# Attention of a two-layer trunk on one core: TensorE's order written out by hand, scores two units ahead, an even fill, the compressed branch in stages

## The chip, the cores and the metric

One core of one Trainium2 chip. The metric is the device time of one execution of the whole kernel, in microseconds (us), the median of several runs. All data are float32; some matmul operands are held as a pair of fp32r tiles ("high" and "low" part), so that a product is taken in three or two passes.

## The reference

Two layers, 256 tokens, width 1024. Layer 0 is native sparse attention, layer 1 an S5 state-space mixer; each is gated by silu(z) and added to the residual stream. Only layer 0 matters here; cut to its core:

```python
q, kc, vc, ks, vs, kw, vw, gates, z = split(rmsnorm(x) @ w_in)   # 16 heads of 64, 4 groups
k_cmp, v_cmp = compress(kc), compress(vc)      # silu(blocks of 32 tokens @ w1) @ w2: 15 blocks
for each block of 64 queries:
    p_c = softmax(q k_cmp - slope * distance)  # compressed branch
    p_s = softmax(q k_sel - slope * distance)  # selected blocks (at 256 tokens: all of them)
    p_w = softmax(q k_win - slope * distance)  # window of 512: all of them
    o = g0 * p_c v_cmp + g1 * p_s v_sel + g2 * p_w v_win
h1 = x + (o * silu(z)) @ w_out
```

Layer 1 then takes `h1` through its own projections and a scan, whose tables depend on its parameters alone ("ep" and "bbT" below) and are made beside the attention.

## The kernel before

**What is computed where.** The query, gate, key and value projections of layer 0 come as jobs of steps: `PRE` (line 36) lists those done ahead of the attention (values, keys, gates, the two inputs of the compression, and the queries q0 of group 0). `FILL` (line 37) lists the jobs that run beside it: the queries q1 to q3, the z gates z0 to z3 (eight steps each, of two fp32 matmuls, 128x256), `m` (the compression's hidden layer, eight steps) and `c` (its output, two steps). A job's name given several times stands for one step at a time, a name given once for all its steps.

**The attention** runs over 24 units (line 1045): 4 groups, 2 pairs of heads, 3 units a pair. Unit u=0 is the first 128 queries of both heads, u=1 and u=2 are the second 128 queries of one head each. Each unit has:

- `scores` (line 933): TensorE multiplies q and k into one of two "su" banks; VectorE adds the distance term and takes the row minimum (L955), ScalarE takes the exponential (L959), GpSimd two small steps on the sums (L964, L965), VectorE the reciprocal (L966), ScalarE scales (L968). The result is `pt`, two buffers.
- `transposes` (line 970): four TensorE transposes of `pt` (L973), copied by VectorE to `pT` (L975, three buffers).
- `values` (line 977): for u=0 and u=2 the products with v (L986) into one "ob" bank; with u=0 also the compressed branch's product (L1005), if its weights are there. Otherwise the pair is put aside by a copy (`aside`, L1012), and `complete` and `gated` finish it later.

The compressed branch of a group (`cmp_branch`, line 890) is scores (L894), a copy to `sct`, transposes of it (L900) and a softmax that goes from VectorE to GpSimd (L906), ScalarE, VectorE, GpSimd (L910), VectorE and GpSimd (L912, L913); `cmp_transpose` (line 916) transposes its result back on TensorE (L919).

**The loop** (lines 1127 to 1141) takes for unit n: the scores of unit n+1, three steps of the background (`adv(PACE)`), fill steps, out-projection steps if the fill is used up (`out_some`), one step of the compressed branch (`cmp_ready`), values of unit n-1, fill again, transposes of unit n. Up to unit 5 there are four fill steps a unit, then three (`RATES`), so the 66 steps are used up some five units before the end.

**The background** (`s5_gen`, line 484) makes layer 1's tables: 24 GpSimd steps for `ep` (lines 567 to 576), then 16 rounds of three GpSimd steps for `bbn` (two buffers), each closed by four TensorE transposes (L604) and a ScalarE copy (L606) in the same step.

**The out-projection** with `w_out0` is 8 steps (first 512 columns: `out_step`; the others: `gen1`) of 12 fp32r matmuls, 128x512. Each needs its weights split by ScalarE (`wh`, L207) and GpSimd (`wl`, L209), and the gated outputs split by `oz_split` (`ozh`, `ozl`, L1038 and L1039). `ozl` takes one of four buffers ("actT") that the normalised input `xn`, which all fill steps read, belongs to as well.

**The order.** Each engine runs its own queue in a fixed order. The order is made ahead of time by a planner: it takes instructions by priority (their place in the program) as soon as its own estimate of times says that they can start. Only inside a block `tc.manual_schedule(engines=...)` do the named engines keep the order of the program. In the kernel before, the attention's loop stands outside such a block; the out-projection's rest (lines 1150 to 1159) stands in one for TensorE.

Of the kernel before, what the change touches and what calls it, by code (L numbers as in the profile page):

```python
# [8 lines left out]
F32 = mybir.dt.float32  # L9
# [24 lines left out]
BGOFF = 0  # L34
WCOL = {"ck": 1024, "cv": 1280, "k0": 1536, "v0": 1792, "k1": 2048, "v1": 2304}
PRE = "v0 v1 k0 k1 gt ck cv q0"
FILL = "q1 q1 m q1 q1 m q1 q1 m q1 q1 m m m m m c z0 q2 z1 q3 z2 z3"
RATES = (4, 3)
SLOT_L = [4 * lh + l4 for l4 in range(4) for lh in range(2)]


# [5 lines left out]
def kernel(  # L47
# [52 lines left out]
    def bank(tag="b1", bufs=None):  # L100
        return phase["pool"].tile([P, 512], F32, tag=tag, name=tag, bufs=bufs or phase["bufs"])
# [4 lines left out]
    def bg_bank():  # L106
        return psb.tile([P, 512], F32, tag="bg", name="bg")
# [32 lines left out]
    def bb_part(g):  # L140
        for g0, t_ in reversed(bbT):
            if g >= g0:
                return t_, g - g0
# [238 lines left out]
    def ptt(o, a, b_, op=ALU.mult):  # L382
        PL.tensor_tensor(o, a, b_, op=op)  # L383
# [100 lines left out]
    def s5_gen():  # L484
# [100 lines left out]
        xp_ = xm.__enter__()  # L585

        GB = 4
        for q in range(GS // GB):
            gs = slice(q * GB, (q + 1) * GB)
            sh = [P, GB, L, 16]  # L590
            bbn = xp_.tile(sh, F32, tag="bbn", name="bbn", bufs=2)
            bbt = xp_.tile(sh, F32, tag="bbt", name="bbt", bufs=1)

            def pb_(ri):
                return pws[:, ri, :, gs].rearrange("p l g -> p g l").unsqueeze(3).to_broadcast(sh)

            ptt(bbn, b1c[:, gs].unsqueeze(2).to_broadcast(sh), pb_(0))
            yield
            ptt(bbt, b2c[:, gs].unsqueeze(2).to_broadcast(sh), pb_(1))
            yield  # L600
            ptt(bbn, bbn, bbt, ALU.add)
            bt = bg_bank()
            for i in range(4):
                T.transpose(bt[:, i * P:(i + 1) * P], bbn[:, i].rearrange("p l c -> p (l c)"), ident)  # L604
            o, g_ = bb_part(q * GB)
            A.activation(o[:, g_:g_ + 4].rearrange("p g x -> p (g x)"), bt, AF.Copy)  # L606
            yield
        xm.__exit__(None, None, None)
        sh_ld["bbar"] = True
        while "taps" not in sh_ld:  # L610
# [36 lines left out]
    def adv(n, offset=BGOFF):  # L647
        with tc.high_priority(-offset):
            for _ in range(n):
                next(bg, None)  # L650
# [103 lines left out]
    def cmp_steps():  # L754

        b = bank("cm", 1)
        for t in range(2):
            T.transpose(b[:, t * P:(t + 1) * P], hid[:, t * P:(t + 1) * P], ident)
        V.tensor_copy(hidT.rearrange("p t v x -> p (t v x)"), b[:, :256])
        b = bank("cm", 1)  # L760
        for t in range(2):
            T.matmul(b[:, :G0 * NB], w2[:, 0, t].rearrange("p u d -> p (u d)"), hidT[:, t, 0],
                     start=(t == 0), stop=(t == 1))
        V.tensor_scalar(kcT[:, :, 0:NB], b[:, :G0 * NB].rearrange("p (g n) -> p g n", n=NB), 0.5, None, op0=ALU.mult)
        dump("kcT", kcT)

        V.tensor_reduce(vm, ident[:R0 * NB, :R0 * NB].rearrange("p (r n) -> p r n", n=NB), axis=AX.X, op=ALU.add)
        V.tensor_scalar(vm, vm, 0.5, None, op0=ALU.mult)
        for t in range(2):
            V.tensor_copy(hidTv4[:, t], hidT[:, t, 1].rearrange("p (g n) -> p g n", n=NB).unsqueeze(2)  # L770
                          .to_broadcast([P, G0, R0, NB]))
        yield
        b = bank("cm", 1)
        for g in range(G0):
            for t in range(2):
                T.matmul(b[:R0 * NB, g * 64:g * 64 + 64], hidTv4[:, t, g].rearrange("p r n -> p (r n)"),
                         w2[:, 1, t, 0], start=(t == 0), stop=(t == 1))
        for r in range(R0):
            V.tensor_scalar(vc2[:, :, r], b[:R0 * NB, :256].rearrange("p (g d) -> p g d", g=G0), vm[:, r:r + 1],
                            None, op0=ALU.mult)  # L780
        dump("vc2", vc2)
        yield
# [85 lines left out]
            done.add(name)  # L868

    n_steps = {}  # L870
    STEPS = {"gt": 8, "v0": 1, "v1": 1, "m": 8, "c": 2}
    for i, name in enumerate(PRE.split()):
        if i == 1:
            b = bank("cm", 1)
# [15 lines left out]
    def cmp_branch(g, qs):  # L890

        b = bank("cm", 1)
        for r in range(R0):
            T.matmul(b[32 * r:32 * r + 32, :S], kcT[:, g], qs[r % 2][:, r // 2].bitcast(F32), start=True, stop=True,  # L894
                     tile_position=(0, 32 * r))
        sct = awp.tile([P, S], F32, tag="sct", name="sct", bufs=1)
        V.tensor_copy(sct, b[:, :S])
        b = bank("cm", 1)
        for j in range(NQ):
            T.transpose(b[:, j * P:(j + 1) * P], sct[:, j * P:(j + 1) * P], ident)  # L900
        sc = awp.tile([P, NQ, R0, NB], F32, tag="sc", name="sc", bufs=2)
        V.scalar_tensor_tensor(sc, b[:, :S].rearrange("p (j r n) -> p j r n", j=NQ, r=R0)[:, :, :, 0:NB], 0.125,
                               cbias[:, :, 4 * g:4 * g + 4], op0=ALU.mult, op1=ALU.add)
        mx = smp.tile([P, NQ, R0], F32, tag="mx", name="mx")
        V.tensor_reduce(mx, sc, axis=AX.X, op=ALU.max)
        PL.tensor_tensor(sc, sc, mx.unsqueeze(3).to_broadcast([P, NQ, R0, NB]), op=ALU.subtract)  # L906
        A.activation(sc, sc, AF.Exp)
        sm = smp.tile([P, NQ, R0], F32, tag="sm", name="sm")
        V.tensor_reduce(sm, sc, axis=AX.X, op=ALU.add)
        PL.tensor_scalar(sm, sm, 1e-30, None, op0=ALU.max)  # L910
        V.reciprocal(sm, sm)
        PL.tensor_tensor(sm, sm, gate[:, :, 4 * g:4 * g + 4], op=ALU.mult)  # L912
        PL.tensor_tensor(sc, sc, sm.unsqueeze(3).to_broadcast([P, NQ, R0, NB]), op=ALU.mult)  # L913
        return sc
# [11 lines left out]
    class Pair:  # L926
# [6 lines left out]
        def scores(self, u):  # L933
# [10 lines left out]
            if u == 0:  # L944
                for hf in range(2):
                    self.b8[hf] = awp.tile([P, S], F32, tag="b8", name="b8", bufs=4)
                    A.activation(self.b8[hf], dist, AF.Copy, scale=-8.0 * _slope(4 * g + 2 * self.pr + hf))
            pt = awp.tile([P, 4, P], F32, tag="pt", name="pt", bufs=2)
            self.pt[u] = pt
            parts = []  # L950
            for i, hf in enumerate(heads):
# [18 lines left out]
        def transposes(self, u):  # L970
            tb = bank("tu", 1)
            for i in range(4):
                T.transpose(tb[:, i * P:(i + 1) * P], self.pt[u][:, i], ident)  # L973
            self.pT[u] = awp.tile([P, 4, P], F32, tag="pT", name="pT", bufs=3)
            V.tensor_copy(self.pT[u].rearrange("p a q -> p (a q)"), tb)  # L975

        def values(self, u, pcT):
# [30 lines left out]
        def aside(self):  # L1008

            i = 2 * self.g + self.pr  # L1010
            part = ozf[:, 6 + i] if i < 2 else awp.tile([P, S], F32, tag="part", name="part", bufs=2)
            A.activation(part, self.ob[:, :S], AF.Copy, scale=0.5)  # L1012
            self.ob, self.half = part, True

# [25 lines left out]

    fill = FILL.split()
    seq = []
    for name in fill:
        seq += [name] * (1 if fill.count(name) > 1 else STEPS.get(name, KT))
    units = [(g, pr, u) for g in range(G0) for pr in range(2) for u in range(3)]
    owed = 0.0
    pairs, cmps, pcT = {}, {}, {}

    def fill_next():
        if seq:  # L1050
            step(seq.pop(0))
# [2 lines left out]
        while key not in done:  # L1054
            fill_next()

    def fill_some(n):
        nonlocal owed
        owed += 0.5 * RATES[n >= 6]
        while owed >= 1.0:  # L1060
            owed -= 1.0
            fill_next()

    def stage_s(n):
        if n < len(units):
            g, pr, u = units[n]
            if u == 0:
                if pr == 0:
                    fill_until(f"q{g}")
                pairs[g, pr] = Pair(g, pr)  # L1070
            pairs[g, pr].scores(u)
# [35 lines left out]
    def cmp_ready(n):  # L1107

        g, pr, u = units[n]
        for c in range(G0):  # L1110
            if c in cmps and c not in pcT:
                pcT[c] = cmp_transpose(cmps[c])
                return
        c = len(cmps)
        if c < G0 and "c" in done and f"q{c}" in done and (c <= g or (c == g + 1 and pr == 1 and u > 0)):
            cmps[c] = cmp_branch(c, qs_of[c])

    def gate_ready():
        for p_ in list(ungated):
# [4 lines left out]
                p_.gated(z_of[p_.g])  # L1124
                gated.add(2 * p_.g + p_.pr)

    fill_some(0)
    fill_some(0)
    stage_s(0)
    for n, (g, pr, u) in enumerate(units):  # L1130
        stage_s(n + 1)
        adv(PACE)
        fill_some(n)
        out_some()
        cmp_ready(n)
        gate_ready()
        if n > 0:
            stage_v(n - 1)
        fill_some(n)
        out_some()  # L1140
        pairs[g, pr].transposes(u)
    while seq:
        fill_next()
    while "bbar" not in sh_ld:
        adv(1)
    for j in range(NQ):
        for l_ in range(4):
            nc.sync.dma_start(h1s[j][32 * l_:32 * l_ + 32], x3[j, l_])
# [391 lines left out]
```

## Time and profile before

| what | value |
|---|---|
| median of 3 runs | 413.19 us (411.97 to 413.63) |
| profiled execution, its own time | 414.05 us |
| profiled execution, span of the trace | 412.3 us |
| mean granted TensorE clock | 0.933 |
| busy: TensorE matmul, GpSimd, VectorE, ScalarE | 354.2, 269.3, 227.9, 178.4 us |

Times are us from the start of the span. PE is TensorE, DVE VectorE, ACT ScalarE, POOL GpSimd, SP the queue that issues most transfers. A name with L is a line of the kernel. An fp32 matmul is recorded as two instructions, so counts of these are twice those in the code; an fp32r matmul is recorded once. The records of one engine overlap a little, so the spacing of starts says more than the duration of one. "Granted clock" is the share of TensorE's full clock: 1.00 is 2.4 GHz and 0.50 is 1.2 GHz.

### The profile page before, as it was taken

Reading aid. Unit: us, or ns where it says so; the run is one execution under the profiler, and the core shown is the slowest. Engines: PE = TensorE matmul, PEld = TensorE weight load, DVE = VectorE, ACT = ScalarE, POOL = GpSimd, SP = SyncE. Lnnn points to the kernel's source line nnn. Section 1 sums busy time; section 2 is a strip of 40 time slices with the busy share of each in tenths; the row PEclk is TensorE's granted clock in tenths of the full one; section 3 lists DMA queues with packets and bytes.
Section 4 is the critical chain, followed back from the end, with each engine's and each line's share of the span. In section 5 each row is a group of like instructions: output and inputs, shape, how many; then the busy total and the mean of one; then the engine's idle time right before and its main releaser. Section 6 shows DMA issues by size and latency. Waiting matters only on the chain.

```text
span 412.3 us, 6834 instructions
## 1 busy us (share of the span) xinstructions
PE 354.2 (86%) x2505; PEld 293.0 (71%) x2505; DVE 227.9 (55%) x582; ACT 178.4 (43%) x397; POOL 269.3 (65%) x281
## 2 busy tenths in 40 slices
PE   3899599999999998968998879994858599999990
PEld 3688468865888787644766657783847599999890
DVE  4969904433355243524555498563999944264243
ACT  3212420145366467566784454342513335444432
POOL 7009459989987789999544489321872476665760
PEclk9699979999999999985999999998696899999996
DMA  8964315558633315411311335996741215655403
GB/s 256 158 172 114 110 53 153 152 190 244 181 103 99 106 57 178 126 52 51 103 36 58 113 103 99 172 87 180 251 156 54 71 34 158 199 163 200 152 2 102
DMA packets 59970, 52.03 MB, mean 126 GB/s; under 512 B 21928, under 2 KB 52704, under 8 KB 59872
## 3 DMA queue, kind: packets, MB, share of 16 engines
q1 hardware_dynamic: 49536, 50.41, 43.9%
q10 hardware_dynamic: 10400, 1.18, 2.2%
q8 instruction: 20, 0.33, 0.4%
q14 instruction: 14, 0.11, 0.1%
HBM read 48.17 MB, written 1.05 MB: 119 GB/s over the span
## 4 chain that ended last, share of the span: by engine, by line
PE 57%; DVE 16%; SPq 6%; POOL 6%; DMA 5%; issue 5%; ACT 3%; DVEq 0%; ACTq 0%; POOLq 0%
PE b L267 16%; SPq L1181 5%; PE b L280 4%; PE b L224 4%; PE b L225 4%; PE b L226 4%; PE ob L986 3%; PE tu L973 2%; PE b L246 2%; PE b L244 2%; PE b L245 2%; DVE pw L377 2%; POOL wl L209 2%; PE cm L745 2%; DVE bbT L1357 2%
## 5 line engine op out<-in xcount | busy, mean ns | idle before, releaser
L209 POOL TENSOR_TENSOR wl<-raw,wh 128x1024 fp32r<-128x1024 f32 x30 | 74.3, 2480 | 48.3 <-ACT wh L207 48.1
L267 PE MATMUL b<-xn,raw 128*128 128x256 f32 (+1 forms) x400 | 94.9, 390 | 4.7 <-DVE kl L795 3.4
L267 PEld LDWEIGHTS b<-xn,raw 128*128 128x128 f32 (+1 forms) x400 | 74.1, 190 | 18.6 <-issue 4.6
L207 ACT ACTIVATE wh<-raw 128x1024 fp32r<-128x1024 f32 x48 | 50.8, 1058 | 67.0 <-PE b L225 20.7
L209 DVE TENSOR_TENSOR wl<-raw,wh 128x1024 fp32r<-128x1024 f32 x18 | 26.3, 1462 | 26.3 <-ACT wh L207 26.3
L959 ACT ACTIVATE pt<-pt,nm 128x128 f32<-128x128 f32 (+1 forms) x64 | 28.3, 444 | 24.8 <-DVE nm L955 24.7
L225 PE MATMUL b<-yl,wh 128*128 128x256 f32 x128 | 36.1, 283 | 0.0
L224 PE MATMUL b<-yh,wh 128*128 128x256 f32 x128 | 36.1, 284 | 0.0
L226 PE MATMUL b<-yh,wl 128*128 128x256 f32 x128 | 36.0, 283 | 0.0
L975 DVE COPY pT<-tu 128x512 f32<-128x512 f32 x24 | 16.6, 691 | 25.4 <-PE tu L973 24.7
L968 ACT ACTIVATE pt<-pt,su 128x128 f32<-128x128 f32 (+1 forms) x64 | 24.6, 443 | 11.6 <-DVE su L966 11.5
L224 PE MATMUL b<-xp,wh 128*128 128x256 f32 x64 | 20.2, 317 | 5.7 <-ACT wh L207 5.7
L224 PEld LDWEIGHTS b<-yh,wh 128*128 128x128 f32 x128 | 24.5, 192 | 0.2 <-issue 0.2
L225 PEld LDWEIGHTS b<-yl,wh 128*128 128x128 f32 x128 | 24.6, 192 | 0.0
L226 PEld LDWEIGHTS b<-yh,wl 128*128 128x128 f32 x128 | 24.5, 192 | 0.0
L383 POOL TENSOR_TENSOR ep<-c1c,pw 128x1024 f32<-128x1024 f32 x8 | 16.0, 2022 | 10.3 <-ACT c1c L546 5.3
L955 DVE CUSTOM_DVE_ANT_0 pt<-su,b 128x128 f32<-128x128 f32 (+1 forms) x64 | 19.4, 351 | 4.7 <-PE su L943 4.7
L226 PE MATMUL b<-xp,wl 128*128 128x256 f32 x64 | 20.1, 316 | 1.6 <-POOL wl L209 1.6
L383 POOL TENSOR_TENSOR bbn<-bbn,bbt 128x512 f32<-128x512 f32 x16 | 20.4, 1274 | 0.6
L383 POOL TENSOR_TENSOR bbn<-b1c,h 128x512 f32<-128x512 f32 x16 | 17.8, 1111 | 4.6 <-PE bg L604 4.4
L986 PE MATMUL ob<-pT,vsw 128*64 128x128 f32 x192 | 17.4, 297 | 3.4 <-DVE pT L975 3.4
L225 PE MATMUL b<-xp,wh 128*128 128x256 f32 x64 | 19.8, 311 | 0.0
(319 smaller groups left out, 874.1 us busy)
## 6 DMA issues: line engine op xcount, KB each, us to landing
raw<-in_l_w_in_dram SPq DMA_DIRECT2D x44, 512.0 KB, 4.0
raw<-in_l_w_out_dram SPq DMA_DIRECT2D x16, 512.0 KB, 3.9
raw<-in_l_w_glu_dram SPq DMA_DIRECT2D x16, 512.0 KB, 3.6
raw<-in_l_cmp_k_w_dram SPq DMA_DIRECT2D x4, 512.0 KB, 3.9
raw<-in_l_cmp_v_w_dram SPq DMA_DIRECT2D x4, 512.0 KB, 3.9
xin<-in_x_dram SPq DMA_DIRECT2D x2, 512.0 KB
h<-in_x_dram SPq DMA_DIRECT2D x8, 128.0 KB, 3.3
tm<-kt__2197 SPq DMA_DIRECT2D x4, 128.0 KB
```

The source lines that it names most:

```text
L207: A.activation(hi, raw, AF.Copy)
L209: lo_eng[-1].tensor_tensor(lo, raw, hi.bitcast(F32), op=ALU.subtract)
L224: T.matmul(dst, a, xh[:, k], start=(k == 0 and e == 0), stop=False)
L225: T.matmul(dst, a, xl[:, k], start=False, stop=False)
L226: T.matmul(dst, b, xh[:, k], start=False, stop=(k == KT - 1 and e == len(dsts) - 1))
L267: T.matmul(dst, w[:, i, e * m:(e + 1) * m], xn[:, k], start=(k == 0 and e == 0), stop=(k == KT - 1 and e == len(dsts) - 1))
L383: PL.tensor_tensor(o, a, b_, op=op)
L955: V.tensor_tensor_reduce(o.rearrange("p t k -> p (t k)"), sb[:, i * w + br * nk:i * w + (br + 1) * nk], self.b8[hf][:, S - nk:S], -0.125, ...
L959: A.activation(o, o, AF.Exp, scale=-1.0, bias=self.nm[:, j, hf, br:br + 1], accum_out=self.su[:, j, hf, br:br + 1])
L968: A.activation(o, o, AF.Copy, scale=r)
L986: T.matmul(self.ob[64 * hf:64 * hf + 64, j * P:(j + 1) * P], vsw[:, kt, br, 64 * g:64 * g + 64], p_, start=first, stop=last, tile_position ...
L1181: nc.sync.dma_start(tm[16 * s_:16 * s_ + 16, 16 * j:16 * j + 16].rearrange("p q l c -> p q (l c)")[:, :, 16 * l_:P], kt_[32 * j:32 * j + 1 ...
```

## The change

- TensorE's instructions of the attention's loop are put into one `manual_schedule` block: they run in the order of the program.
- Scores are taken two units ahead (`AHEAD = 2`), ahead of the first fill step; `pt` has three buffers, `pT` two.
- `FILL` gives the number of steps with each name; the rate is 2.75 steps a unit throughout, in two portions. 67 steps (`c` has three) are used up in the last unit, so no out-projection step falls into the loop. `m` and `q1`, and `c` and `q2`, are mixed.
- `cmp_branch` ends with the copy to `sct`; the transposes and the softmax (`cmp_probs`) come a unit later, `cmp_transpose` a unit after that. `cmp_steps` has one more break.
- The transposes and the copy that close a background round come a round later (`bbar_out`), ahead of the last GpSimd step of the next. `adv(PACE)` moves behind `cmp_ready` and `gate_ready`.
- Four instead of two of the halves put aside live in `ozf`.

```diff
-FILL = "q1 q1 m q1 q1 m q1 q1 m q1 q1 m m m m m c z0 q2 z1 q3 z2 z3"
-RATES = (4, 3)
+FILL = "q1 2 m 1 q1 2 m 1 q1 2 m 1 q1 2 m 5 q2 2 c 1 q2 2 c 1 q2 2 c 1 q2 2 z0 8 q3 8 z1 8 z2 8 z3 8"
+RATE = 2.75
+AHEAD = 2
...
+        def bbar_out(q, bbn):
+            bt = bg_bank()
+            for i in range(4):
+                T.transpose(bt[:, i * P:(i + 1) * P], bbn[:, i].rearrange("p l c -> p (l c)"), ident)
+            o, g_ = bb_part(q * GB)
+            A.activation(o[:, g_:g_ + 4].rearrange("p g x -> p (g x)"), bt, AF.Copy)
...
+            if q > 0:
+                bbar_out(q - 1, prev)
             ptt(bbn, bbn, bbt, ALU.add)
-            bt = bg_bank()
-            for i in range(4):
-                T.transpose(bt[:, i * P:(i + 1) * P], bbn[:, i].rearrange("p l c -> p (l c)"), ident)
-            o, g_ = bb_part(q * GB)
-            A.activation(o[:, g_:g_ + 4].rearrange("p g x -> p (g x)"), bt, AF.Copy)
+            prev = bbn
             yield
+        bbar_out(GS // GB - 1, prev)
...
         V.tensor_copy(sct, b[:, :S])
+        return sct
+
+    def cmp_probs(g, sct):
         b = bank("cm", 1)
...
-            pt = awp.tile([P, 4, P], F32, tag="pt", name="pt", bufs=2)
+            pt = awp.tile([P, 4, P], F32, tag="pt", name="pt", bufs=3)
...
-            self.pT[u] = awp.tile([P, 4, P], F32, tag="pT", name="pT", bufs=3)
+            self.pT[u] = awp.tile([P, 4, P], F32, tag="pT", name="pT", bufs=2)
...
-            part = ozf[:, 6 + i] if i < 2 else awp.tile([P, S], F32, tag="part", name="part", bufs=2)
+            part = ozf[:, 6 + i % 2] if i in (0, 1, 4, 5) else awp.tile([P, S], F32, tag="part", name="part", bufs=2)
...
         for c in range(G0):
+            if c in scts and c not in cmps:
+                cmps[c] = cmp_probs(c, scts[c])
+                return
             if c in cmps and c not in pcT:
                 pcT[c] = cmp_transpose(cmps[c])
                 return
...
-    fill_some(0)
-    fill_some(0)
-    stage_s(0)
-    for n, (g, pr, u) in enumerate(units):
-        stage_s(n + 1)
-        adv(PACE)
-        fill_some(n)
-        out_some()
-        cmp_ready(n)
-        gate_ready()
-        if n > 0:
-            stage_v(n - 1)
-        fill_some(n)
-        out_some()
-        pairs[g, pr].transposes(u)
-    while seq:
-        fill_next()
-    while "bbar" not in sh_ld:
-        adv(1)
+    with tc.manual_schedule(engines={E_.PE}):
+        for n in range(AHEAD):
+            stage_s(n)
+            fill_some()
+        for n, (g, pr, u) in enumerate(units):
+            stage_s(n + AHEAD)
+            fill_some()
+            out_some()
+            cmp_ready(n)
+            gate_ready()
+            adv(PACE)
+            if n > 0:
+                stage_v(n - 1)
+            fill_some()
+            out_some()
+            pairs[g, pr].transposes(u)
+        while seq:
+            fill_next()
+        while "bbar" not in sh_ld:
+            adv(1)
```

## Rows read from the trace of the kernel before

**Rows 1.** The page: TensorE's busy tenths and granted clock (PEclk, tenths) in 40 slices.

```profile
PE   3899599999999998968998879994858599999990
PEclk9699979999999999985999999998696899999996
```

**Rows 2.** Busy by stretch, from q0's end to the out-projection's end: length, PE, PEld, DVE, ACT, POOL, clock, DMA share, GB/s.

```profile
79.00:110.00 31.00, 29.99 (x172) 21.43 (x171) 10.98 (x40) 12.95 (x43) 28.12 (x21) 1.00 0.67 205
110.00:150.00 40.00, 40.00 (x262) 33.54 (x261) 17.34 (x64) 22.24 (x66) 31.97 (x42) 1.00 0.35 95
150.00:178.00 28.00, 26.64 (x176) 20.92 (x175) 12.31 (x42) 19.76 (x53) 27.20 (x31) 1.00 0.40 128
178.00:197.00 19.00, 13.85 (x68) 8.57 (x67) 6.00 (x26) 11.59 (x35) 18.10 (x26) 0.64 0.17 60
197.00:222.00 25.00, 22.42 (x152) 15.74 (x151) 13.63 (x58) 19.20 (x64) 11.62 (x25) 1.00 0.20 62
222.00:238.00 16.00, 14.04 (x76) 10.52 (x78) 9.77 (x20) 6.28 (x12) 7.74 (x3) 1.00 0.32 99
```

**Rows 3.** The same columns, one short stretch inside the fourth of those.

```profile
184.00:187.00 3.00, 1.97 (x8) 1.57 (x8) 0.62 (x2) 1.32 (x3) 2.84 (x4) 0.50 0.00 0
```

**Rows 4.** Groups of POOL instructions, 150 to 200 us: busy us, mean ns, idle before.

```profile
L209 POOL TENSOR_TENSOR wl<-raw,wh 128x1024 fp32r<-128x1024 f32 x5 | 11.8, 2368 | 0.1
L383 POOL TENSOR_TENSOR bbn<-bbn,bbt 128x512 f32<-128x512 f32 x8 | 10.2, 1276 | 0.1
L1039 POOL TENSOR_TENSOR ozl<-ozf,ozh 128x256 fp32r<-128x256 f32 x4 | 2.9, 734 | 0.2
```

**Rows 5.** PE's timeline in the out-projection (start, length), spacing of one matmul.

```profile
225.27 0.39 PE L246 MATMUL su<-wh,ozl 128*128 128x512 f32 x1
226.86 0.39 PE L244 MATMUL b<-wh,ozh 128*128 128x512 f32 x1
```

**Rows 6.** Groups of PE instructions, 79 to 222 us: fill, hidden layer, values.

```profile
L267 PE MATMUL b<-xn,raw 128*128 128x256 f32 x224 | 52.9, 381 | 1.3 <-DVE qs L828 1.3
L745 PE MATMUL cm<-raw,bbT 128*64 128x256 f32 x64 | 9.9, 389 | 1.0 <-DMA raw<-in_l_cmp_k_w_dram 0.6 <-DMA raw<-in_l_cmp_v_w_dram 0.4
L986 PE MATMUL ob<-pT,vsw 128*64 128x128 f32 x178 | 16.3, 298 | 2.6 <-DVE pT L975 2.6
```

**Rows 7.** Timelines of ACT, DVE and PE: q0's split, first scores to first transposes.

```profile
78.94 1.20 ACT L826 ACTIVATE qs<-b 64x512 fp32r<-64x512 f32 x2 [16.18 <-PE b L267]
80.17 1.41 DVE L828 TENSOR_TENSOR qs<-b,qs 64x512 fp32r<-64x512 f32 x2 [4.80 <-ACT qs L826]
85.28 0.39 PE L942 MATMUL su<-kh,qs 128*128 128x256 f32 x1
92.92 2.08 ACT L968 ACTIVATE pt<-pt,su 128x128 f32<-128x128 f32 x6 [1.73 <-DVE su L966]
```

**Rows 8.** PE's and POOL's timelines: compressed branch of three groups, L900 to L913.

```profile
125.80 0.38 PE L900 MATMUL cm<-ident,sct 128*128 128x128 f32 x2
133.01 0.40 POOL L913 TENSOR_TENSOR sc<-sc,sm 128x128 f32<-128x128 f32 x1
148.77 0.38 PE L900 MATMUL cm<-ident,sct 128*128 128x128 f32 x2
159.75 0.39 POOL L913 TENSOR_TENSOR sc<-sc,sm 128x128 f32<-128x128 f32 x1
197.82 0.38 PE L900 MATMUL cm<-ident,sct 128*128 128x128 f32 x2
203.14 0.41 POOL L913 TENSOR_TENSOR sc<-sc,sm 128x128 f32<-128x128 f32 x1
```

**Rows 9.** Busy by stretch, columns as in Rows 2: a wait ahead of the attention.

```profile
47.00:50.50 3.50, 0.15 (x2) 0.00 (x0) 3.33 (x12) 2.64 (x5) 1.88 (x1) 0.87 0.40 136
50.50:53.00 2.50, 2.42 (x6) 1.26 (x7) 1.76 (x6) 0.00 (x0) 2.50 (x3) 0.50 0.00 0
53.00:56.00 3.00, 3.00 (x8) 1.43 (x7) 0.00 (x0) 0.00 (x0) 1.59 (x1) 0.50 0.00 0
```

More of the change, by code (lines that the diff above doesn't have):

```diff
@@ L759, in cmp_steps @@
         V.tensor_copy(hidT.rearrange("p t v x -> p (t v x)"), b[:, :256])
+        yield
         b = bank("cm", 1)
@@ L870 @@
     n_steps = {}
-    STEPS = {"gt": 8, "v0": 1, "v1": 1, "m": 8, "c": 2}
+    STEPS = {"gt": 8, "v0": 1, "v1": 1, "m": 8, "c": 3}
     for i, name in enumerate(PRE.split()):
@@ L1042 @@
     seq = []
-    for name in fill:
-        seq += [name] * (1 if fill.count(name) > 1 else STEPS.get(name, KT))
+    for name, n_ in zip(fill[::2], fill[1::2]):
+        seq += [name] * int(n_)
     units = [(g, pr, u) for g in range(G0) for pr in range(2) for u in range(3)]
     owed = 0.0
-    pairs, cmps, pcT = {}, {}, {}
+    pairs, scts, cmps, pcT = {}, {}, {}, {}
     def fill_next():
@@ L1055, in fill_until, with fill_some @@
             fill_next()
-    def fill_some(n):
+    def fill_some():
         nonlocal owed
-        owed += 0.5 * RATES[n >= 6]
+        owed += 0.5 * RATE
         while owed >= 1.0:
@@ L1115, in cmp_ready @@
         if c < G0 and "c" in done and f"q{c}" in done and (c <= g or (c == g + 1 and pr == 1 and u > 0)):
-            cmps[c] = cmp_branch(c, qs_of[c])
+            scts[c] = cmp_branch(c, qs_of[c])
     def gate_ready():
```

## The prediction, made before the changed kernel ran

> **What bounds the kernel now.** I read the page's slices first [rows 1]: TensorE is busy nine tenths or more for most of the span, so time is to be won only where a slice falls below nine or where the clock falls below full. For the stretch that the change rewrites, from the end of q0 to the end of the out-projection, the table by stage [rows 2] gives both. From 79 to 238 us TensorE is busy 146.9 of 159 us: 12.1 us are waits. In the fourth stage the granted clock is 0.64, and inside it there are moments at 0.50 [rows 3], the lower of the two levels; a mean of 0.64 means that 72% of those 19 us ran at half speed, which cost half of 0.72 x 13.85 = 5.0 us. So the same instructions at full clock without a wait are 146.9 - 5.0 = 141.9 us, and the most that a better order can give is 159 - 141.9 = **17.1 us**. The reader is to see where it lies: 79 to 178 us hold only 2.4 us of waits, 178 to 222 us hold 7.7 us and the whole clock loss. That is the stretch in which the fill is nearly used up, then gone, and GpSimd is full: 18.1 of 19 us [rows 2], with five weight splits of the out-projection and four splits of its input between the background's steps [rows 4].
>
> **What moves.** The work of each engine stays the same, apart from a few copies. With 48 of the out-projection's matmuls, at 0.227 us by their spacing [rows 5], in the loop of before (three `out_step`s and the first of `gen1`), a unit costs TensorE (132.9 - 5.0 - 10.9) / 24 = 4.9 us of the busy time up to 222 us. After, these matmuls follow the loop; that is the same work in another place and counts nothing by itself. The sum is therefore 141.9 us plus the waits W of the new order, against 159: the change gains 17.1 - W.
>
> **The waits of the new order, one by one.**
>
> *The start, 5.6 us.* Before, TensorE went from q0 into q1 and `m` at once. Now the block's first instruction is the scores of unit 0, and it needs q0's split: ScalarE starts on it at 78.94, VectorE ends at 81.58 [rows 7], 2.6 us in which every fill step is queued behind the scores. The next wait is at unit 0's transposes. From the first scores at 85.28 to the four scaled tiles (four of the six at 92.92, so 94.3) the chain through DVE, ACT, POOL, DVE, ACT took 9.0 us [rows 7]; ahead of the transposes TensorE now has three scores (four matmuls' worth of 0.227 at most, some 0.5 each) and five fill steps of 0.9 (52.9 us for 56 steps [rows 6]), 6.0 us in all. That leaves 3.0 us. All 24 units' work is queued behind both. Ends: 2.6 and 8.
>
> *Transposes later on, nothing.* From the third unit on, three units (14.7 us) lie between scores and transposes, against the 9.0 us chain; this cover is what `AHEAD` and the third `pt` buffer buy. With one unit less it would be 9.8 us, and nothing left for a busy GpSimd.
>
> *The compressed branch, 3.6 us.* The transposes of the result (L919) now stand one unit behind those of the scores (L900), and TensorE waits there if the softmax isn't through; fill and scores are queued behind. The interval holds a unit with the heavier values, so I estimate it at 5.3 rather than 4.9 us. The chain took 7.6, 11.4 and 5.7 us for three of the groups [rows 8], which would mean waits of 2.3, 6.1 and 0.4 us, four times. The first two passed with background steps between its GpSimd steps, the second also with weight splits (2.37 us each [rows 4]); the third when the background was done. After, no weight split falls into the loop while fill is left, and the chain stands ahead of its own unit's background steps in priority; I take 0.9 us a group, nearer to the third row. Ends: 0 and 24.
>
> *The background's transposes, nothing.* In program order TensorE may meet a round whose GpSimd sum isn't there yet. They stand a round later now, and GpSimd has room: of its 105.4 busy us between 79 and 197 [rows 2] the five weight splits (11.8) and four input splits (2.9 [rows 4]) leave the loop. A round costs it at most 3.8 us (three steps, 1.28 us the longest) and the unit's small sums, against 4.9 on TensorE. Ends: 0 and the 8 us in which GpSimd stood idle from 110 to 150.
>
> *Loads, 1.0 us.* The two waits for `m`'s weights [rows 6] may stay; the mixed list asks for them more slowly (2.75 steps a unit, not four), but in a fixed order nothing passes them. Ends: 0 and 2. The out-projection's loads are issued later on SP, as z2 and z3 free their buffers; the first two land beside units 20 to 23, so I cost them at nothing.
>
> *Values behind their copies, 0.8 us.* The 2.6 us of before [rows 6] fell where no fill was left. One or two fill steps (0.9 to 1.8 us) now stand between transposes and values everywhere. Ends: 0 and 3.
>
> *The out-projection, 2.0 us.* The last stage of before waits 16 - 14.0 us [rows 2]. It now has eight steps on end instead of four. `ozl` shares a buffer with `xn`, which the last z3 step reads, so all its pieces come at the end: eight of 0.73 us and the weight splits of 2.37 us [rows 4] against 2.7 us of matmuls a step (12 x 0.227). GpSimd can split two or three weights ahead, and 0.73 us serves 1.4 us of matmuls, so I leave it at 2.0. Ends: 0 and 6.
>
> **Sum.** W = 5.6 + 3.6 + 1.0 + 0.8 + 2.0 = 13.0 us, the gain 17.1 - 13.0 = 4.1 us. The span goes from 412.3 to 408.2, the profiled execution from 414.05 to about 410. That execution lies 0.9 us over the median of 413.19, from which I take the same 4.1: **409.1 us**. What follows the stretch (scan and gated unit) starts earlier by as much; nothing in it waits for something that the change leaves where it was.
>
> **The clock** was left out of W. Ahead of the attention, a stretch with only 0.15 us of matmuls in 3.5 us is followed by 0.50 for at least 5.5 us [rows 9]; 5.4 busy us at half speed cost 2.7. The waits at the start, 2.6 and 3.0 us with 6 us of work between, are a little shorter. The Trainium skill, "TensorE: Matmul & The Clock Gate", section "HAM oscillation — how this bites in real kernels", holds that an engine which waits between bursts of work is throttled anew for each burst; by it the fixed order would pay at every wait. Rows 3 and 9 agree with it for one wait each; the short waits up to 178 us left the clock at 1.00 [rows 2], which speaks for at most the two longest.
>
> **Rivals.** *Slower, by the compressed branch.* If GpSimd goes on placing background steps into the softmax, the wait per group is the mean of the three rows, 2.9 us: W = 13.0 + 8.0 = 21.0, 3.9 us slower, **417.1**; at the mean of the first two (4.2) it is 422.3. For: two of three rows had it, and GpSimd stays nearly full. Against: the splits go, the priority turns. It decides from 1.9 us a group, a chain of 7.2 us. *No change, by the clock.* One fall costs 2.7 (411.8), two 5.4 (414.5): about **413**. For: rows 9. Against: the waits are shorter than that one. *Nearly no waits.* Softmax in time, the first transposes late by nothing, loads in time: W = 2.6 + 0.4 x 4 + 0.8 + 1.0 = 6.0, **402.1**. For: in the dense stretch from 110 to 150 us TensorE waited for nothing with the planner's order either. Against: the 9.0 us chain at the start. *The order changes nothing*, since the planner's was near it already: then the spread of the fill alone counts; it lies within the first case.
>
> **Chances.** The forecast, W from 10 to 16 us (406 to 412): 0.38. Compressed branch: 0.25. Clock: 0.17. Nearly no waits: 0.20. Range 400 to 421: below it W under 4 and above it a softmax at the second row's pace or two rivals together, some 0.15 in all. A measurement of this kernel tells about 0.5% (2.1 us) from no change. Faster by more: 0.20 + most of 0.38, 0.55; within: 0.19; slower: 0.26.
>
> **What would show it.** Right: no idle slice between 178 and 222 us and a clock of 1.00 there; TensorE idle for 2.6 us ahead of the first scores, released by VectorE's L828, and some 3 us ahead of the first transposes, released by ScalarE's L968; at L919 four waits of about 1 us; the out-projection's 96 matmuls on end. Wrong: waits at L919 over 2 us or at L604 at all, a clock of 0.50 after 82 us, or a GpSimd that is late with `ozl` and `wl` behind the loop by more than 2 us.

## The result, and the profile after

The changed kernel takes **427.89 us** (median of 4 runs, 424.37 to 430.86) against 413.41 us for the kernel before (4 runs, 411.97 to 414.68): a ratio of 1.033, 95% interval 1.029 to 1.036. The ratio leaves out the slowest of the four, 430.86 us, as a slow run; the two medians alone give 1.035. It is slower by 14.5 us, where 409.1 was forecast, and it lies outside the range of 400 to 421 as well. The profiled execution is the quickest of the four, 424.37 us with a span of 422.6 and a mean granted clock of 0.935; the others had clocks of 0.921 to 0.925. So the profile shows 10.3 of the 14.5 us (422.6 against 412.3).

TensorE's work is the same, 355.0 busy us against 354.2. The stretch from q0's end to the end of the out-projection took 79 to 249.5 us, before 79 to 238: 11.5 us more, and the rest of the span 1.2 us less. In the prediction's terms W is 170.5 - 141.9 = **28.6 us** instead of 13.0. The table by stage of after (columns as in [rows 2]) says where:

```profile
79.00:110.00 31.00, 27.43 (x180) 19.28 (x179) 13.68 (x60) 19.82 (x67) 28.39 (x25) 1.00 0.53 166
110.00:150.00 40.00, 37.05 (x258) 28.82 (x257) 21.02 (x74) 26.41 (x84) 32.22 (x46) 0.96 0.25 72
150.00:178.00 28.00, 22.38 (x122) 16.15 (x121) 11.47 (x47) 14.41 (x47) 16.98 (x29) 0.88 0.21 56
178.00:197.00 19.00, 16.77 (x117) 12.81 (x117) 7.79 (x31) 12.14 (x37) 15.81 (x23) 1.00 0.20 56
197.00:222.00 25.00, 18.04 (x104) 14.53 (x104) 5.43 (x16) 9.87 (x24) 13.92 (x14) 0.86 0.55 148
222.00:250.00 28.00, 25.60 (x143) 19.75 (x146) 12.10 (x23) 11.91 (x20) 21.69 (x17) 1.00 0.43 137
```

Set against [rows 2], the fourth stage, the one the change was to mend, is mended: 2.2 us idle instead of 5.2, at full clock instead of 0.64. But the stretch from 79 to 178 us, which held 2.4 us of waits, now holds 12.1 (3.6 + 2.9 + 5.6), and the fifth stage 7.0 instead of 2.6. All six add up to 23.7 idle us; the missing 4.9 us of W are busy time beyond the 141.9, for the most part clock (see below). The list of what TensorE waited for in this stretch (line waited at, releaser, its line: us in all, times, longest) accounts for nearly all of the 23.7:

```profile
PE cm L932 <- POOL sc L926: 7.3, 4, 3.2
PE bg L594 <- ACT bbT L596: 7.0, 1, 7.0
PE su L955 <- DVE qs L838: 2.3, 2, 2.0
PE b L248 <- POOL ozl L1052: 2.1, 2, 1.7
PE cm L1018 <- DVE pcT L934: 1.5, 3, 0.5
PE cm L754 <- DMA raw<-in_l_cmp_v_w_dram: 0.9, 2, 0.5
PE cm L904 <- DVE su L979: 0.8, 1, 0.8
PE cm L1018 <- DVE part L1031: 0.5, 1, 0.5
PE cm L1018 <- DVE ozf L1031: 0.5, 1, 0.5
...
PE ob L999 <- DVE pT L988: 0.3, 1, 0.3
```

Lines have moved with the change: L932 is before's L919 (the result's transposes), L926 is L913, L594 and L596 are L604 and L606 (the background's transposes and their copy), L955 is L942, L1018 is L1005.

**First row: the compressed branch.** Of one group, TensorE's timeline (start, length, engine, line; in brackets the wait ahead and its releaser) shows transposes in, transposes back:

```profile
146.72 0.38 PE L913 MATMUL cm<-ident,sct 128*128 128x128 f32 x2
154.61 0.41 PE L932 MATMUL cm<-ident,sc 128*64 128x128 f32 x2 [3.21 <-POOL sc L926]
```

and GpSimd's timeline what its four softmax steps (L919, L923, L925, L926) stood behind:

```profile
148.01 0.84 POOL L1037 TENSOR_TENSOR ozf<-ozf 128x256 f32<-128x256 f32 x1
148.82 1.09 POOL L385 TENSOR_TENSOR bbn<-b1c,h 128x512 f32<-128x512 f32 x1
149.88 0.40 POOL L919 TENSOR_TENSOR sc<-sc,mx 128x128 f32<-128x128 f32 x1
...
150.66 1.27 POOL L385 TENSOR_TENSOR bbn<-bbn,bbt 128x512 f32<-128x512 f32 x1
...
152.16 0.24 POOL L923 TENSOR_SCALAR sm<-sm 128x8 f32<-128x8 f32 x1
152.49 1.10 POOL L385 TENSOR_TENSOR bbt<-h 128x512 f32<-128x512 f32 x1
153.55 0.20 POOL L925 TENSOR_TENSOR sm<-sm,gate 128x8 f32<-128x8 f32 x1
...
154.15 0.40 POOL L926 TENSOR_TENSOR sc<-sc,sm 128x128 f32<-128x128 f32 x1
```

Three background steps of 1.1 to 1.3 us, and at the start one product of the gated outputs (L1037), stand between or ahead of softmax steps of 0.2 to 0.4. VectorE had the first step's input ready at 147.8 us; GpSimd came to it at 149.88. No weight split is there, as foreseen, and yet this chain took 7.8 us (146.72 to 154.55), the others 6.6, 6.6 and 7.5. That is near the first group of [rows 8], 7.6, and none is as short as the third, 5.7.

**Second row: the background's last round.** TensorE's timeline again:

```profile
203.48 0.60 PE L594 MATMUL bg<-ident,bbn 128*128 128x128 f32 x4
211.04 1.08 PE L594 MATMUL bg<-ident,bbn 128*128 128x128 f32 x4 [6.96 <-ACT bbT L596]
```

The last two rounds follow each other with nothing between them, both through the one "bg" bank, so the last one needs ScalarE's copy of the one before. ScalarE's timeline shows where that copy (L596) was:

```profile
207.28 1.06 ACT L209 ACTIVATE wh<-raw 128x1024 fp32r<-128x1024 f32 x1 [3.50 <-DMA raw<-in_l_w_out_dram]
...
210.32 0.57 ACT L596 ACTIVATE bbT<-bg 128x512 f32<-128x512 f32 x1
```

TensorE's results were there at 204; the copy is queued behind a split of an out-projection weight that had not landed, and then behind the exponentials that the split had delayed. The chain of work that ended last goes through that load:

```profile
200.61 6.64 DMA raw<-in_l_w_out_dram
```

By this chain it took 6.6 us, beside eight loads of 128 KB for the next stage; the profile's list of transfers gives the four loads of this kind in that stretch a median of 3.6.

### The profile page after: what moved, and what is told of

Same layout as the page of the kernel before. It is cut to its first block, busy times and chain, and to the rows that moved or that the text cites. A ratio compares the mean times of both kernels' runs of the same rounds, so it can differ in the third digit from the quotient of the medians.

```text
span 422.6 us, 6835 instructions
## 1 busy us (share of the span) xinstructions
PE 355.0 (84%) x2505; PEld 294.0 (70%) x2505; DVE 230.7 (55%) x582; ACT 179.8 (43%) x401; POOL 273.3 (65%) x285
## 4 chain that ended last, share of the span: by engine, by line
PE 43%; POOL 25%; DVE 11%; issue 7%; ACT 5%; DMA 5%; SPq 3%; DVEq 0%; POOLq 0%; ACTq 0%
PE b L269 8%; POOL ep L385 8%; PE b L282 4%; PE b L228 4%; PE b L226 4%; PE b L227 4%; POOL bbn L385 4%; POOL et L385 4%; SPq L1198 3%; PE b L248 2%; PE b L246 2%; POOL bbt L385 2%; PE b L247 2%; POOL wl L211 2%; POOL tm L1192 2%
## 5 line engine op out<-in xcount | busy, mean ns | idle before, releaser
L269 PE MATMUL b<-xn,raw 128*128 128x256 f32 (+1 forms) x400 | 100.6, 398 | 3.4 <-DVE kl L805 3.4
L269 PEld LDWEIGHTS b<-xn,raw 128*128 128x128 f32 (+1 forms) x400 | 74.6, 193 | 19.9 <-issue 7.0
L211 DVE TENSOR_TENSOR wl<-raw,wh 128x1024 fp32r<-128x1024 f32 x18 | 27.2, 1512 | 23.1 <-ACT wh L209 23.1
L385 POOL TENSOR_TENSOR ep<-c1c,pw 128x1024 f32<-128x1024 f32 x8 | 16.0, 2020 | 10.3 <-ACT c1c L548 5.3
L385 POOL TENSOR_TENSOR ep<-ep,et 128x1024 f32<-128x1024 f32 x8 | 18.9, 2364 | 0.4
```

What stands on the lines that cost most here:

```text
L211: lo_eng[-1].tensor_tensor(lo, raw, hi.bitcast(F32), op=ALU.subtract)
L269: T.matmul(dst, w[:, i, e * m:(e + 1) * m], xn[:, k], start=(k == 0 and e == 0), stop=(k == KT - 1 and e == len(dsts) - 1))
```

## The experiments

Every variant starts from the changed kernel unless it says otherwise. Two lines inserted further up shift later names by two in some of them (L934 is L932, L928 is L926). Times are medians; ratios are to the kernel before, run beside them (413.2 to 413.4 us).

**e1: the change without the fixed order.** The loop's block is taken away; rates, `AHEAD` and the stages of the compressed branch stay.

```diff
-    with tc.manual_schedule(engines={E_.PE}):
+    with ExitStack():
```

> The changed kernel with the loop outside the block: the planner orders TensorE again; the even fill, scores two ahead and the stages stay. Theory A (the fixed order turns lateness of other engines into waits of TensorE: 7.3 us for the softmax of the compressed branch, 7.0 us at the last round of the background, 2.6 us at the completions, and some 6 us of half clock behind them): most of it goes, about 413 us. Theory B (the fill that lasts to the end and the out-projection moved behind the loop cost by themselves, whatever the order): 422 us or more.

Measured: 418.83 us, ratio 1.013 (1.008 to 1.017). It lies between the two theories: the fixed order costs 9.1 us of the 14.5, and the rest of the change costs 5.4 with the planner's order. Two stages of its table:

```profile
150.00:178.00 28.00, 27.75 (x177) 22.23 (x176) 13.07 (x53) 20.51 (x59) 23.14 (x28) 1.00 0.44 143
178.00:197.00 19.00, 11.71 (x55) 6.73 (x56) 5.68 (x23) 10.19 (x32) 18.27 (x28) 0.78 0.00 0
```

The hole is where it was before [rows 2]: TensorE full up to 178 us, then 7.3 of 19 us idle beside a GpSimd that is full, 18.3. The planner doesn't keep the spread that the rates ask for: no fill matmul (L269) runs after 178 us here, where the changed kernel has them up to 222.

**e2: the split behind the copies.** The `wh` splits of the out-projection's first weights (`split`) are kept behind the last L596 in ScalarE's queue.

```diff
...
-        A.activation(hi, raw, AF.Copy)
+        with (tc.issue_after(hold[0]) if hold else ExitStack()):
+            A.activation(hi, raw, AF.Copy)
...
+    hold.append(sh_ld["bb_act"].ins)
...
```

> The changed kernel with ScalarE's splits of the out-projection's first weights queued behind its last copy of a background round, so that none of them can stand ahead of that copy and wait for its load. Theory A: the 7.0 us wait at the background's last transposes and the half clock behind it (2.5 us) go, 427.9 - 9 = 419 us. Rival: the splits, now late, are waited for behind the loop instead; within 3 us of 427.9.

Measured: 421.67 us, ratio 1.019 (1.014 to 1.024), 6.2 us less than the changed kernel. The wait at the last round goes from 7.0 to 2.6 us; the four at L932 stay at 7.3. So the late weight did hold the copy, and its 4.4 us were worth 6.2. What is left, 2.6 us, is the two rounds on end: TensorE is through with the first at 205.2 us, and the copy stands behind a unit's exponentials until 207.08.

**e3: the compressed branch one unit later.** The transposes back come one unit after they came before.

```diff
...
             if c in cmps and c not in pcT:
+                if c not in rest:
+                    rest.add(c)
+                    break
                 pcT[c] = cmp_transpose(cmps[c])
```

> The changed kernel with one more unit between the softmax of the compressed branch and the transposes of its result. Theory A: the four waits at these transposes (7.3 us) and the half clock after three of them (3 to 4 us) go, less up to 1.5 us for two more completions: about 418 us. Rival: GpSimd is the bound and TensorE's wait moves to the background's transposes; within 3 us of 427.9.

Measured: **412.86 us** (10 runs), ratio 0.998 (0.996 to 1.001): 15.0 us less (418 were expected), from an edit that takes away 7.3 us of waits. No wait at L932 is left, and the clock from 150 to 178 us is 1.00 instead of 0.88. In the profiled executions the stretch up to the end of the out-projection is 12.6 us shorter: besides these 7.3 us, the wait at the last round is 3.1 us shorter, and TensorE's busy time falls by 2.3, which I put down to the clock; the completions wait much as before (2.9 us, 2.5 in the changed kernel). The last round still waits, but for something else; TensorE's timeline:

```profile
190.42 0.60 PE L594 MATMUL bg<-ident,bbn 128*128 128x128 f32 x4
194.90 1.12 PE L594 MATMUL bg<-ident,bbn 128*128 128x128 f32 x4 [3.88 <-POOL bbn L385]
```

GpSimd's timeline shows a weight split and two output products (L1037) inside the last round's three steps:

```profile
188.01 2.38 POOL L211 TENSOR_TENSOR wl<-raw,wh 128x1024 fp32r<-128x1024 f32 x1
...
190.78 1.10 POOL L385 TENSOR_TENSOR bbn<-b1c,h 128x512 f32<-128x512 f32 x1
191.83 1.65 POOL L1037 TENSOR_TENSOR ozf<-ozf 128x256 f32<-128x256 f32 x2
...
193.59 1.26 POOL L385 TENSOR_TENSOR bbn<-bbn,bbt 128x512 f32<-128x512 f32 x1
```

**e4: e2 and e3 together.** 

> Both edits. If the two causes are separate the gains add: about 409 us, under the kernel before. If one only hides the other, 417 us or more.

Measured: 411.67 us (10 runs), ratio 0.995 (0.993 to 0.998), 1.2 us less than e3, which is within their intervals, where e2 alone gave 6.2. The wait at the last round is the same 3.9 us as in e3, for GpSimd. So with the compressed branch out of the way the late weight no longer ends that wait; what makes it is that the two rounds stand on end, and either ScalarE or GpSimd is late for the second.

**e5: e3, and the last round three steps later.** Three more steps of the background without work stand ahead of the last round's transposes, so that a unit's work lies between the two rounds.

```diff
+        for _ in range(3):
+            yield
         bbar_out(GS // GB - 1, prev)
```

> The kernel of the later compressed branch (412.9 us) with the transposes of the background's last round one unit later; until now they stand right behind those of the round before, with nothing between. Theory A: the one long wait left in its loop (3.9 us at these transposes) and the half clock behind it (2 to 3 us) go: about 407 us. Rival: GpSimd is late with its queue as a whole, the wait moves to the next thing that needs it: 411 us or more.

Measured: **404.53 us** (401.42 to 407.20), ratio 0.978 (0.973 to 0.983). This beats both kernels, the one before by 2.2% (1.7 to 2.7). Two stages of its table:

```profile
178.00:197.00 19.00, 19.00 (x131) 15.68 (x130) 7.74 (x34) 13.08 (x39) 17.14 (x24) 1.00 0.44 137
197.00:222.00 25.00, 23.93 (x124) 18.60 (x123) 8.48 (x19) 11.07 (x18) 24.20 (x16) 1.00 0.50 171
```

TensorE idles 1.1 us from 178 to 222, where before [rows 2] had 7.7 us and the slow clock. GpSimd is as full as it ever was, 17.1 of 19 and 24.2 of 25 us, and TensorE waits for it only once there, for 0.4 us (a piece of `ozl`).

**e12: the last round later, alone.** The edit of e5 without that of e3.

> The changed kernel (427.9 us) with nothing but the last round of the background one unit later. Theory A: the 7.0 us wait and the 2.5 us of half clock behind it go, but the scales of the last units still stand behind the same late load on ScalarE and 2 to 3 us come back: about 421 us. Rival: the wait is set by the load and only moves: 425 us or more.

Measured: 421.82 us, ratio 1.020 (1.010 to 1.030): 6.1 us less than the changed kernel. The two waits of TensorE that matter:

```profile
PE cm L934 <- POOL sc L928: 7.3, 4, 3.2
...
PE bg L594 <- ACT bbT L596: 0.5, 1, 0.5
```

The second falls from 7.0 to 0.5, the first doesn't move. With e3 (15.0) the two make 21.1 us, and together in e5 they made 23.4. So the two holes are separate causes, and closing both undoes the whole loss and gives 9 us more.

**e6: before with the block alone.** The loop of the kernel before is put under `manual_schedule`, nothing else.

> The kernel before with nothing but the loop put into the block that fixes TensorE's order. Theory A (a fixed order lays every softmax and every copy open that stands right ahead of its user): many more waits than in the changed kernel, since scores are one unit ahead and the compressed branch is one piece: 440 us or more. Rival (the planner's order was near the program's): 413 to 420 us.

Measured: 435.69 us, ratio 1.054 (1.051 to 1.057), the slowest of all, between the theory (440 or more) and its rival. Its two longest waits:

```profile
PE cm L919 <- POOL sc L913: 12.9, 3, 7.9
PE tu L973 <- ACT pt L968: 3.9, 2, 2.3
```

The first had one of 7.9 us, and GpSimd's timeline shows two weight splits inside that softmax:

```profile
197.43 2.36 POOL L209 TENSOR_TENSOR wl<-raw,wh 128x1024 fp32r<-128x1024 f32 x1
...
201.32 2.34 POOL L209 TENSOR_TENSOR wl<-raw,wh 128x1024 fp32r<-128x1024 f32 x1
```

The fill is nearly used up by then (four steps are left when the wait ends at 208.5), so the out-projection's splits already lie in the loop. The second row is the unit's own chain with scores one unit ahead.

**e9 and e10: e5 without one of its other parts.** e9 sets scores one unit ahead, e10 takes the rates of before (four fill steps a unit up to unit 5, then three).

```diff
-AHEAD = 2
+AHEAD = 1
```

> The fastest kernel so far (404.5 us: later compressed branch, later last round) with scores one unit ahead instead of two. Theory A (in a fixed order the 9 us chain from scores to transposes must be covered; two units of 4.9 us hardly do): waits at the transposes in the first units and wherever the background is full, 408 to 416 us. Rival: one unit ahead is cover enough, within 3 us of 404.5.

```diff
...
-        owed += 0.5 * RATE
+        owed += 0.5 * (4, 3)[n >= 6]
...
```

> The same kernel with the rates of before (four steps a unit, then three; the fill ends five units early). With the two long waits gone, the even fill shows what it is worth: if units without fill are exposed in a fixed order, 408 to 414 us; if not, within 3 us of 404.5.

Measured: e9 418.36 us, ratio 1.013 (1.008 to 1.019); e10 426.44 us, ratio 1.029 (1.023 to 1.035). Both are above what was expected. So beside e5 the second unit of scores is worth 13.8 us and the even fill 21.9. In e9, 8.0 us more are idle from 79 to 222 us than in e5 (15.3 against 7.3), in many waits of 1 to 2.6 us. The transposes, where the theory had put them, make up 1.8 us of it; the others are at the compressed branch, the completions and loads, and why they grow wasn't followed. In e10 one wait stands out; TensorE's timeline, then GpSimd's:

```profile
211.04 0.64 PE L934 MATMUL cm<-ident,sc 128*64 128x128 f32 x2 [5.63 <-POOL sc L928]
```

```profile
201.26 4.19 POOL L1054 TENSOR_TENSOR ozl<-ozf,ozh 128x256 fp32r<-128x256 f32 x6
...
207.07 2.34 POOL L211 TENSOR_TENSOR wl<-raw,wh 128x1024 fp32r<-128x1024 f32 x1
```

As in e6: fill at an end, 6.5 us of the out-projection's splits inside the last group's softmax, so the old rates open the first hole again. From 197 to 222 us 7.8 us are idle at a clock of 0.73; waits for loads of the hidden layer's weights, which the quicker fill asks for sooner, take 4.0 us instead of 1.8. That is a good part of the 21.9, not all of it; the rest wasn't followed.

**e8: the changed kernel with the rates of before.** The edit of e10 without those of e5.

> The changed kernel with the rates of before, four steps a unit up to unit 5, then three, so that the fill ends some five units early and out-projection steps fall into the loop again. Theory A (softmax and last round are what costs; the even fill is worth little by itself): the softmax waits shrink a little under four steps and the last units wait more: 422 to 432 us. Theory B (the even fill and the out-projection behind the loop are the cost): 418 us or less.

Measured: 428.9 us, ratio 1.036 (1.032 to 1.040), against 427.89: no difference. The even fill is worth nothing while the two holes are open, and 21.9 us once they are closed.

**e11: e5 without the fixed order.** The edit of e1 on e5.

> The same kernel with the loop outside the block, ordered by the planner. If the fixed order itself gives the gain once its two holes are closed: 412 us or more, near the 418.8 of the changed kernel without the block. If the stages and the even fill give it: within 3 us of 404.5.

Measured: 412.14 us (10 runs), ratio 0.997 (0.994 to 1.001). The fixed order, which cost 9.1 us in the changed kernel, gains 7.6 us here. One stage of its table:

```profile
178.00:197.00 19.00, 15.76 (x105) 9.80 (x103) 10.48 (x49) 13.70 (x48) 18.02 (x31) 1.00 0.08 29
```

It is the hole of [rows 2] again, 3.2 us of it, and 4.5 us from 197 to 222.

**e7: e5 and three more edits.** Two fill steps ahead of the first scores, `gate_ready` ahead of `cmp_ready` (the completions one unit later), and the scan's `memset` on GpSimd behind the last `ozl`.

```diff
...
+            if n == 0:
+                fill_next()
+                fill_next()
             stage_s(n)
...
-            cmp_ready(n)
             gate_ready()
+            cmp_ready(n)
...
-    PL.memset(tm, 0.0)
+    with tc.issue_after(sh_ld["ozl"].ins):
+        PL.memset(tm, 0.0)
```

> The kernel of the run before last (later compressed branch, last round later) with two fill steps ahead of the first scores (2.3 us of waits), the completions a unit behind the weights that they need (2.9 us) and GpSimd's clearing of a large tile queued behind the last split of the out-projection's input (1.7 us). Theory A: the waits add, 407 - 6 = about 401 to 403 us. Rival: the end is set by GpSimd or by loads, 406 us or more.

Measured: 405.84 us (6 runs), ratio 0.983 (0.981 to 0.986), not told apart from e5; the 401 to 403 us expected were missed. The wait at the start fell from 2.3 to 0.6 us, but the loads of the hidden layer's weights then cost 2.8 us instead of 1.8, and a score of the compressed branch waited 1.8 us for `vc`. The wait for `ozl` (2.1 us in e5) is gone, but the completions still wait. So the order moved up into other waits.

Not tried by themselves: the third `pt` buffer against one less of `pT`, the mixed list of fill, the later `adv(PACE)`, and the stages of the compressed branch without the block.

## Why the prediction was wrong

**What bounds the kernel: right.** The sum 141.9 + W holds, as the work was unchanged, and most of the 17.1 us was there to be had: in e5 the stretch runs from 77.2 to 230.2 us, so W is 153.0 - 141.9 = 11.1, with waits still left at the start, at completions and at loads. (Its busy time there is 141.9 us, the sum's own figure. Its span is 404.8 us, 7.5 less than before: 6.0 in the stretch, 1.7 ahead of it, where nothing was edited.) The forecast W of 13.0 is near what e5 reaches, not what the change does.

**The compressed branch: the term that was mis-sized.** 0.9 us a group was taken, 3.6 in all. Measured were 1.15, 3.21, 0.88 and 2.07 us, together 7.3, a mean of 1.8. Of the three rows of [rows 8] I chose the third, on the ground that no weight split falls into the loop and that priority puts the softmax ahead of its unit's background steps. The first ground held for these four chains only: splits did fall into the loop while fill was left (GpSimd's at 196.62, 205.86 and 208.41 us, ScalarE's at 202.72 and 207.28), and ScalarE's are what the last round met. The second ground was wrong: three background steps stood among the softmax steps of each group. A place further up in the program doesn't help a step whose input isn't there yet. In the group shown above the steps at 150.66 and 152.49 began before the softmax step's input was there (150.98 and 152.64), and ahead of the first hand-over even steps that began after it (148.01 and 148.82) went first, since the planner had put them there. The first row, with background steps alone between, was the case to take; it gives 2.3. ([rows 8] leaves out the fourth chain of before, from 171.77 to 188.95 us, 17.2 us with two weight splits in it; it would have moved the rival's mean up, not the choice.) The rival "slower by the compressed branch" named this, with 1.9 us as the point from which it decides.

**What that term brought with it was left out.** The completions (L1018) were not in the sum: with the pairs put aside until the branch is through, they now follow the transposes back at once, and their three rows in the list make 2.5 us, besides 0.8 at L904. And two of the four clusters of waits cost clock. That e3 closes 7.3 us of waits and gives 15.0 isn't owed to the completions, which wait for 2.9 us there: in the profiled executions 3.1 us more come from the last round and 2.3 from busy time, and the rest of the 15.0 they don't show.

**The background's transposes: the step that failed outright.** They were costed at nothing, because a round takes GpSimd 3.8 us against 4.9 on TensorE. That holds for the mean, and GpSimd was indeed not the bound. But the last round has no unit in front of it: in the program's order its transposes follow those of the round before directly, and in one bank. Two more things were missed: the bank is freed by ScalarE, in whose queue the out-projection's first splits stand, and these wait for loads that I had costed at nothing "beside units 20 to 23". It cost 7.0 us and a fall of the clock; e12 gives 6.1 us back. The end of 8 us that I kept for this term (GpSimd's idle time) had the size, from another mechanism.

**The clock: left out of W, and it fell three times.** Three pairs of stretches of after, each the waits and what follows (columns as in [rows 2]):

```profile
132.00:136.00 4.00, 1.96 (x7) 0.79 (x7) 1.52 (x9) 2.82 (x13) 1.31 (x5) 0.94 0.47 131
136.00:139.00 3.00, 3.00 (x15) 2.22 (x15) 0.42 (x1) 0.60 (x1) 1.78 (x2) 0.51 0.00 0
150.00:156.00 6.00, 2.28 (x13) 1.38 (x11) 2.69 (x14) 3.79 (x15) 4.22 (x10) 1.00 0.33 87
156.00:162.00 6.00, 5.48 (x21) 3.52 (x20) 0.85 (x2) 0.84 (x2) 2.69 (x3) 0.50 0.00 0
207.00:211.00 4.00, 0.00 (x0) 0.00 (x0) 0.00 (x0) 3.72 (x10) 3.71 (x3) 0.53 0.76 216
211.00:214.00 3.00, 2.96 (x21) 2.33 (x21) 0.17 (x1) 0.80 (x2) 0.26 (x2) 0.50 0.73 211
```

Half of the 11.4 busy us at half clock is 5.7 us. That is an estimate; W has 4.9 beyond the idle time, of which 0.5 is the end of q0, at 79.5 here. My argument was that only the two longest waits, those at the start, could bring a fall. They brought none; the falls came behind the compressed branch, twice, and behind the last round. The rule of the Trainium skill that I quoted, "TensorE: Matmul & The Clock Gate", section "HAM oscillation — how this bites in real kernels", that an engine which waits between bursts is throttled anew (told there of a loop that waits for loads), described these falls better than my reading of [rows 2]: the trace shows the clock at 0.50 to 0.53 behind each of these three. But it doesn't hold at every wait, so the sum couldn't have been made by it: behind the 2.0 us at the start the clock stayed at 1.00, and so it did behind the wait of the fourth group (2.07 us):

```profile
192.50:195.70 3.20, 0.97 (x8) 0.70 (x7) 0.99 (x8) 3.20 (x12) 2.48 (x7) 1.00 0.39 148
195.70:198.00 2.30, 2.30 (x16) 1.64 (x17) 0.00 (x0) 1.57 (x5) 2.30 (x2) 1.00 0.04 7
```

What decides between them stays open.

**The terms that were near.** The start: 2.3 us at the first scores against 2.6, but nothing at the first transposes, where 3.0 was set, as GpSimd and ScalarE were quicker than in [rows 7]; 2.3 against 5.6 in all. Loads 0.9 against 1.0, values 0.3 against 0.8, out-projection 2.1 (the wait for `ozl`) against 2.0. Transposes later on waited for nothing, as said; with one unit less (e9) they wait for 1.8 us, so this cover by itself doesn't explain the 13.8 us that the second unit of scores is worth.

**In one sum:** start -3.3, branch +3.7, completions and L904 +3.3, last round +7.0, loads -0.1, values -0.5, out-projection +0.1, clock +4.9: 15.1 of the 15.6 us by which W exceeds the forecast; the other 0.5 are two short waits outside its terms (0.3 at L1223, 0.2 at L1018 for ScalarE). The profile doesn't hold the other 4.2 us of the medians' difference: the median of the changed kernel lies 3.5 us above its profiled execution, that of the kernel before 0.6 below its own. The other executions of the changed kernel ran at a lower mean clock; where, stays open.

## What to carry to other kernels

A fixed order on the engine that bounds the kernel turns every lateness of another engine into a stop for all that is queued behind, so what it pays depends on the cover of each hand-over: here it cost 9.1 us with two of them open and gained 7.6 with both closed. Look for the one place that has no cover (the last round, the one-bank pair), since an average says nothing of it. Cost such a hand-over by the row of its chain in which the other engine was as busy as it will be (the first of [rows 8] gives 2.3 us a group where 1.8 were measured; the slowest, 6.1, would have been far off), ask for every instruction what stands ahead of its releaser in that engine's queue, loads included, and keep an allowance for the slow clock behind it. Two holes and a good spread can hide each other: the even fill was worth 0 with the holes open and 21.9 us with them closed, so parts of such a change are to be tried together as well as alone.

## What the runs showed of the hardware that was not expected

Several short waits close together were followed by half clock: from 132 to 136 us TensorE was busy for 1.96 us, without a single wait of over 1.15 us, and the next 3 us ran at 0.51. Behind the 3.2 us wait the half clock lasted through 156 to 162 us, longer than the wait. The wait of 2.0 us at the first scores (79.5 to 81.5) and the one of 2.07 us at the fourth group (up to 194.6) were followed by work at 1.00. So neither the longest wait nor the sum of waits told alone whether the clock would fall.

Nor does the spread of a kernel's executions follow its waits: four of the changed kernel lie within 1.5% (mean clocks of 0.921 to 0.935), four of e5, which waits far less, within 1.4%, and four of e6, which waits the most, within 0.6%.
